# Feed-forward of a decoder step: the group of two, its PSUM readers and the places of its jobs

## The chip, the cores and the metric

The kernel runs on one core of one Trainium2 chip. The metric is the device time of one execution in microseconds (us), as the median over runs.

## What is computed

One step of a decoder of four layers over 544 columns (512 prompt tokens, 8 requests of 4 new tokens), in fp32. Each layer is a token mixer (convolution, latent attention, retention, convolution) and a gated feed-forward part, each behind an rmsnorm and with a residual add. The change touches the feed-forward part alone:

```python
def _swiglu(h, w1, w3, w2):
    return (jax.nn.silu(h @ w1) * (h @ w3)) @ w2
xp = xp + _swiglu(_rmsnorm(xp, norm_ffn[i]), ffn_w1[i], ffn_w3[i], ffn_w2[i])   # D_MODEL 1024, D_FF 2816
```

Here `w1` is the gate, `w3` the value and `w2` the down product.

## The kernel before, in words

`x` is held transposed in SBUF, 8 tiles of 128 rows by 544 columns. Every fp32 product is made of three matmuls of rounded halves: a weight tile is split by ACT into `wh` (a cast, L485) and by DVE into `wl` (a subtraction, L473), and the product is high by high, low by high and high by low.

The feed-forward part of a layer (`ffn`) is written as one list of **jobs**. A job is one product with all that belongs to it: a load, `sums` (DVE, sums of weight blocks, L580), `high` (the ACT cast of its weights), `low` (the DVE subtraction), `run` (the matmuls) and `after` (the instructions that read its PSUM result). `step(i)` emits job i: loads for job i+6, sums for i+3, its matmuls, then the cast for job i+2, the readers of job i-1, the low half for job i+2. A job with `soon` set has its own readers emitted at the end of its own step; one with `late` set has the readers of the job ahead of it emitted first. `in_order` keeps PE, DVE and ACT in exactly the order in which the jobs are emitted.

The 22 blocks of 128 hidden units are worked off as: four in the plain way (`plain`), their down product, a group of four (`quad`), then in the loop of `ffn` the four jobs of the down product of that group with the 14 jobs of a **group of two** between them, then two more groups of four with their down products. A `quad` group makes 7 products in place of 8 (Strassen's scheme, `four`), once for the gate and once for the value. In the order of the jobs these are products 1, 5, 6, 3, 7, 2, 4 of the scheme:

- The first three write PSUM and are copied to SBUF by ACT (L587: `u1`, `p5`, `u2`). The others go through `put`: for the gate an add on DVE (L638) and a Silu on ACT (L640), for the value an add and a multiplication on DVE (L650, L652), a cast `gh` on ACT (L653) and, one step later, `gl` on DVE.
- Product 6 adds onto the PSUM place of product 1, product 3 onto that of product 5, product 7 onto that of product 6. So each of them has to wait until the reader of the earlier one is done.
- In the group of two (`nt=1`) a job has 12 matmuls and its PSUM places are the two banks of one tile (`pair`): products 1, 6, 7, 4 in bank 0, products 5 and 3 in bank 1. In a group of four (`nt=2`) a job has 24 matmuls and the two places are two tiles. A job of the down product has 48 matmuls (24 ahead of each of its two adds into `x`, L299).

Below, the jobs of the group of two are called job 1 to job 14 (gate 1 to 7, value 8 to 14), the four down jobs between them D1 to D4, and the jobs of the next group of four, which follow, Q1, Q2, Q3, Q4. Before, the order is D1, jobs 1 to 4, D2, jobs 5 to 8, D3, jobs 9 to 11, D4, jobs 12 to 14, Q1. All four layers have this stretch once.

The functions that the diff touches:

Of the kernel before, what the change touches and what calls it, by code (L numbers as in the profile page):

```python
# [136 lines left out]
class Trunk:  # L137
# [306 lines left out]
    def ffn(self, l, last, order):  # L444
# [15 lines left out]
        with ExitStack() as es:  # L460
# [14 lines left out]
            class Job:  # L475

                load = sums = high = low = after = fill = staticmethod(lambda: None)
                late = soon = False

            def weights(job, src, nk, w):  # L480

                def high():
                    job.w = tuple(self.wsp.tile([P, 1024], FR, tag="ws", name="w" + n)[:, :nk * w]
                                  .rearrange("p (k c) -> p k c", k=nk) for n in "hl")
                    nc.scalar.copy(job.w[0], src())  # L485
                job.high, job.low = high, lambda: low(job.w[1], src(), job.w[0])
# [60 lines left out]
            def product(out, c, w, first):  # L547
                wh, wl = w
                bh, bl = blocks[c]
                for t in range(wh.shape[-1] // P):  # L550
                    m = slice(t * P, (t + 1) * P)
                    for i, (a, b) in enumerate(((wh, bh), (wh, bl), (wl, bh))):
                        for k in range(4):
                            nc.tensor.matmul(out[:, t, :HF], lhsT=a[:, k, m], rhs=b[:, k, :],  # L554
                                             start=(first and i == 0 and k == 0), stop=(i == 2 and k == 3),
                                             skip_group_check=True)

            def four(w, f, put, nt):

                a, ps, kept = {}, {}, {}  # L560
                v = lambda x: x[:, :, :HF]

                def load():
                    if nt == 1:
                        for i, n in enumerate(("1", "2")):
                            r = bp.tile([P, 1024], F, tag="A", name="raw", bufs=4).rearrange("p (k c) -> p k c", k=4)
                            nc.sync.dma_start(r, w[:, i * 4:(i + 1) * 4, f * P:f * P + 256])
                            a["1" + n], a["2" + n] = r[:, :, :P], r[:, :, P:]
                        return
                    r = self.rawp.tile([P, 2048], F, tag="raw", name="raw").rearrange("p (k c) -> p k c", k=4)  # L570
                    nc.sync.dma_start(r, w[:, 0:4, f * P:f * P + 512])
                    a["11"], a["21"] = r[:, :, :256], r[:, :, 256:]
                    for i, n in enumerate(("22", "12")):
                        a[n] = bp.tile([P, 1024], F, tag="A", name="raw", bufs=4).rearrange("p (k c) -> p k c", k=4)
                        nc.sync.dma_start(a[n], w[:, 4:8, f * P + 256 - 256 * i:f * P + 512 - 256 * i])

                def whole(out, op, x, y):
                    def sums():
                        a[out] = self.xsp.tile([P, 1024], F, tag="xs", name="S")[:, :nt * 512].rearrange("p (k c) -> p k c", k=4)
                        op(a[out], a[x], a[y])  # L580
                    return sums
                add, sub = nc.vector.tensor_add, nc.vector.tensor_sub

                def copy(name, p):
                    def after():
                        t = kept[name] = self.scr(name).rearrange("p (t n) -> p t n", t=2)[:, :nt]
                        nc.scalar.copy(t, v(ps[p]))  # L587
                    return after

                for c, n, sums, p, first, after in (  # L590
                        ("1", "11", None, "x2", True, copy("u1", "x2")),
                        ("5", "S1", whole("S1", add, "21", "22"), "x3", True, copy("p5", "x3")),
                        ("6", "S2", whole("S2", sub, "S1", "11"), "x2", False, copy("u2", "x2")),
                        ("3", "S4", whole("S4", sub, "12", "S2"), "x3", False, lambda: put("12", v(ps["x3"]), kept["u2"])),
                        ("7", "S3", whole("S3", sub, "11", "21"), "x2", False, lambda: put("22", v(ps["x2"]), kept["p5"])),
                        ("2", "12", None, "x1", True, lambda: put("11", v(ps["x1"]), kept["u1"])),
                        ("4", "22", None, "x2", False, lambda: put("21", v(ps["x2"]), None))):
                    job = Job()
                    if c == "1":
                        job.load = load  # L600
                    if sums:
                        job.sums = sums
                    weights(job, lambda n=n: a[n], 4, nt * P)

                    def run(job=job, c=c, p=p, first=first):
                        if first and nt == 1:
                            if p != "x3":
                                ps["pair"] = self.pair(p)
                            i = int(p == "x3")
                            ps[p] = ps["pair"][:, i:i + 1]  # L610
                        elif first:
                            ps[p] = (self.duo if p == "x2" else self.pair)(p)
                        product(ps[p], c, job.w, first)
                    job.run, job.after = run, after
                    yield job

            def quad(f, gs, nt=2):
# [24 lines left out]
                def value(which, ps, add):  # L642
# [12 lines left out]
                    if which == "21":  # L655
                        gs.extend((G[p][0][:, j, :], G[p][1][:, j, :]) for p in "12" for j in range(nt))
                yield from four(w1, f, gate, nt)
                yield from four(w3, f, value, nt)


# [52 lines left out]
            jobs, gs = [], []  # L713
# [5 lines left out]
            while f < FF // P:  # L719
                gs, ahead = ahead, []  # L720
                jobs.extend(quad(f, gs))
                f += 4
                if last and f == FF // P:
                    break
                back = list(down(f0, f - f0, gs))
                if f0 == 4:
                    two = list(quad(f, ahead, 1))
                    for i, n in enumerate((4, 4, 3, 3)):
                        jobs.append(back[i])
                        jobs.extend(two[:n])  # L730
                        del two[:n]
                    f0, f = f, f + 2
                else:
                    jobs.extend(back)
                    f0 = f
# [14 lines left out]
            def made(i, *what):  # L750
                for n in what:
                    if i < len(jobs) and (i, n) not in done:
                        done.add((i, n))
                        getattr(jobs[i], n)()

            def caught_up():
                todo, behind[:] = behind[:], []
                for x in todo:
                    x()

            def step(i):
                job = jobs[i]
                made(i + 6, "load")
                made(i + 3, "sums")
                if job.late:
                    jobs[i - 1].after()
                    caught_up()
                job.run()
                caught_up()
                made(i + 2, "high")  # L770
                if i and not job.late and not jobs[i - 1].soon:
                    jobs[i - 1].after()
                made(i + 2, "low")
                if job.soon:
                    job.after()
                job.fill()
            for i in range(6):
                made(i, "load")
            for i in range(3):
                made(i, "high", "low")  # L780
            step(0)
            with self.in_order(mybir.EngineType.PE, mybir.EngineType.DVE, mybir.EngineType.Activation):
                for i in range(1, len(jobs)):
                    step(i)
                if not jobs[-1].soon:
                    jobs[-1].after()
                caught_up()
# [1151 lines left out]
```

## Time and profile before

| | |
|---|---|
| median of 3 runs | 2788.76 us (2784.15 to 2789.15) |
| profiled execution | 2775.68 us, span of its instructions 2773.8 us |
| mean granted TensorE clock | 0.994 |
| PE busy | 2707.9 us, 98% of the span |
| DVE, ACT busy | 1942.5 us (70%), 1196.7 us (43%) |
| this stretch in the first layer | job 1 starts at 351.34 us, Q3 at 400.38 us |

PE is the engine of the matmuls, PEld its weight loads, DVE the vector engine, ACT the scalar engine. A row of a timeline has its start in the span, its duration, the engine, the line, the operation, what it writes and reads, and in brackets how long the engine was idle before it and what ended that. PE rows overlap, since matmuls are pipelined: from start to start is what one costs.

### The profile page before, as it was taken

The page shows a single profiled execution, that of the slowest core. Times are in us where ns is not written, and L with a number is a line of the kernel's source. Part 1 is how long each engine was busy: PE and PEld are TensorE (multiplying, and loading weights), DVE is VectorE, ACT ScalarE, POOL GpSimd, SP SyncE. Part 2 cuts the span into 40 slices and gives each one's busy share as a digit, 9 for nine tenths or more (in the row PEclk, how much of TensorE's full clock was granted, in tenths as well). Part 3 has the DMA queues.
Part 4 walks back from the last instruction along what each step waited for, and adds up shares of the span by engine and source line. Part 5 has one row for each costly group of instructions (what it writes and reads, how often), then busy time and mean ns, then how long its engine had stood idle before and what let it go on. Part 6 is the DMA issues. An engine that isn't in the chain of part 4 may idle for free.

```text
span 2773.8 us, 52206 instructions
## 1 busy us (share of the span) xinstructions
PE 2707.9 (98%) x22294; PEld 2544.2 (92%) x22294; DVE 1942.5 (70%) x2878; ACT 1196.7 (43%) x1793; POOL 138.1 (5%) x233
## 2 busy tenths in 40 slices
PE   8999999999899999999999999999999999999998
PEld 7989999997679999999888888899999998999998
DVE  6987765776665867677656565786767798776576
ACT  4155443444454344344534343534434425444345
POOL 1000000021430000000101000000000000000000
PEclk9999999999999999999999999999999999999999
DMA  5544223233333233322525343422331453422322
GB/s 161 184 136 138 92 88 96 91 91 116 87 114 107 77 92 100 99 69 87 194 94 178 109 163 122 142 94 92 96 103 63 128 192 128 143 84 88 98 82 86
DMA packets 222300, 312.47 MB, mean 113 GB/s; under 512 B 15295, under 2 KB 153868, under 8 KB 222038
## 3 DMA queue, kind: packets, MB, share of 16 engines
q1 hardware_dynamic: 209164, 266.84, 30.4%
q0 software_dynamic: 12608, 40.44, 4.2%
q8 instruction: 175, 2.87, 0.4%
q10 hardware_dynamic: 298, 1.88, 0.2%
q14 instruction: 55, 0.45, 0.1%
HBM read 278.78 MB, written 30.85 MB: 112 GB/s over the span
## 4 chain that ended last, share of the span: by engine, by line
PE 89%; DVE 6%; ACT 2%; DMA 1%; issue 1%; another core or an unknown queue 0%; ACTq 0%; DVEq 0%
PE x L554 26%; PE p L216 24%; PE pg L216 7%; PE pqk L216 3%; PE pa L216 3%; PE pwo L216 3%; PE po L216 2%; PE pw L216 2%; PE pd L216 2%; PE pv L1586 1%; PE pv L1587 1%; PE pv L1588 1%; PE ob L1821 1%; DVE cc L881 1%; DMA raw<-in_ffn_w 1%
## 5 line engine op out<-in xcount | busy, mean ns | idle before, releaser
L485 ACT CAST wh<-raw 128x1024 fp32r<-128x1024 f32 (+2 forms) x244 | 239.2, 980 | 365.8 <-PE p L216 200.5
L554 PE MATMUL x<-Bh,wh 128*128 128x272 f32 x2016 | 336.8, 289 | 11.0 <-ACT u L587 5.8
L554 PE MATMUL x<-Bh,wl 128*128 128x272 f32 x2016 | 334.6, 288 | 0.0
L554 PE MATMUL x<-Bl,wh 128*128 128x272 f32 x2016 | 334.5, 288 | 0.0
L473 DVE TENSOR_TENSOR wl<-raw,wh 128x1024 fp32r<-128x1024 f32 (+2 forms) x244 | 276.4, 1133 | 76.5 <-ACT wh L485 74.5
L196 ACT CAST wh<-raw 128x1024 fp32r<-128x1024 f32 (+2 forms) x170 | 160.6, 948 | 367.5 <-PE pg L216 77.8
L554 PEld LDWEIGHTS x<-Bh,wh 128*128 128x128 f32 x2016 | 283.9, 188 | 15.2 <-ACT u L587 7.6
L216 PE MATMUL p<-gl,wh 128*128 128x272 f32 x1344 | 296.0, 288 | 1.0 <-DVE gl L473 1.0
L216 PE MATMUL p<-gh,wh 128*128 128x272 f32 x1344 | 296.9, 289 | 0.0
L216 PE MATMUL p<-gh,wl 128*128 128x272 f32 x1344 | 296.2, 288 | 0.0
L554 PEld LDWEIGHTS x<-Bh,wl 128*128 128x128 f32 x2016 | 283.9, 188 | 0.0
L554 PEld LDWEIGHTS x<-Bl,wh 128*128 128x128 f32 x2016 | 283.9, 188 | 0.0
L485 ACT CAST wh<-S 128x1024 fp32r<-128x1024 f32 (+1 forms) x160 | 154.6, 966 | 268.1 <-PE p L216 139.2
L299 DVE TENSOR_TENSOR x<-p,x 128x544 f32<-128x544 f32 x152 | 109.9, 723 | 191.6 <-PE p L216 191.4
L197 DVE TENSOR_TENSOR wl<-raw,wh 128x1024 fp32r<-128x1024 f32 (+2 forms) x170 | 185.4, 1094 | 72.3 <-ACT wh L196 52.9
L473 DVE TENSOR_TENSOR wl<-S,wh 128x1024 fp32r<-128x1024 f32 (+1 forms) x160 | 178.1, 1115 | 71.2 <-ACT wh L485 71.2
L216 PEld LDWEIGHTS p<-gl,wh 128*128 128x128 f32 x1344 | 218.1, 188 | 1.9 <-DVE gl L473 1.9
L216 PEld LDWEIGHTS p<-gh,wh 128*128 128x128 f32 x1344 | 218.0, 188 | 1.2 <-ACT gh L518 0.9
L216 PEld LDWEIGHTS p<-gh,wl 128*128 128x128 f32 x1344 | 217.2, 189 | 0.0
L216 PE MATMUL pg<-xs,wh 128*128 128x272 f32 x1024 | 178.8, 292 | 5.1 <-ACT wh L196 5.1
L216 PE MATMUL p<-xs,wh 128*128 128x272 f32 x1024 | 172.6, 290 | 5.6 <-DVE t L295 5.6
L216 PEld LDWEIGHTS pg<-xs,wh 128*128 128x128 f32 x1024 | 147.7, 190 | 13.2 <-issue 7.3
(540 smaller groups left out, 5323.7 us busy)
## 6 DMA issues: line engine op xcount, KB each, us to landing
raw<-in_ffn_w SPq DMA_DIRECT2D x78, 1024.0 KB
raw<-in_ffn_w SPq DMA_DIRECT2D x88, 512.0 KB
raw<-in_conv_w_pw SPq DMA_DIRECT2D x28, 1024.0 KB
state<-in_state_ret SPq DMA_DIRECT2D x32, 512.0 KB
out_ret_state_sample<-state POOLq DMA_DIRECT2D x32, 512.0 KB
S<-ud SPq DMA_DIRECT2D x48, 280.0 KB
raw<-in_ffn_w SPq DMA_DIRECT2D x16, 768.0 KB
raw<-in_ret_w_v SPq DMA_DIRECT2D x8, 1024.0 KB
```

Source lines behind the costliest of these rows:

```text
L196: self.nc.scalar.copy(hv, raw)
L197: self.nc.vector.tensor_sub(lv, raw, hv.bitcast(F))
L216: nc.tensor.matmul(ps[:M, h, :HF], lhsT=w[:, k, :], rhs=x[:, h * HF:(h + 1) * HF], start=(j == 0 and i == 0), stop=(j == n - 1 and i == 2))
L299: self.nc.vector.tensor_add(x, ps[:, :, :HF], x)
L473: nc.vector.tensor_sub(out, a, flat(h))
L485: nc.scalar.copy(job.w[0], src())
L554: nc.tensor.matmul(out[:, t, :HF], lhsT=a[:, k, m], rhs=b[:, k, :], start=(first and i == 0 and k == 0), stop=(i == 2 and k == 3), skip_gr ...
L881: nc.vector.scalar_tensor_tensor(out=cc[m][:, a:z], in0=U[:, m, k + a:k + z], scalar=taps[:, m, k:k + 1], in1=cc[m][:, a:z], op0=ALU.mult, ...
L1586: nc.tensor.matmul(out, lhsT=ah, rhs=bh, start=start, stop=False)
L1587: nc.tensor.matmul(out, lhsT=ah, rhs=bl, start=False, stop=False)
L1588: nc.tensor.matmul(out, lhsT=al, rhs=bh, start=False, stop=stop)
L1821: nc.tensor.matmul(s["ob"][q * 32:(q + 1) * 32, :], lhsT=s["qm"][:, e, q * 2 + r, :], rhs=ts[q // 2][:, q % 2, :], start=(q > 0 and r == 0 ...
```

## The change

It does two things. Jobs of a group of two get a flag `short`, and where the job ahead is `short`, its readers are emitted ahead of the cast for job i+2 instead of behind it. And the 14 jobs stand 5, 4, 3, 2 behind D1, D2, D3, D4, where they stood 4, 4, 3, 3.

```diff
-                late = soon = False
+                late = soon = short = False
...
-                    job.run, job.after = run, after
+                    job.run, job.after, job.short = run, after, nt == 1
                     yield job
...
-                    for i, n in enumerate((4, 4, 3, 3)):
+                    for i, n in enumerate((5, 4, 3, 2)):
                         jobs.append(back[i])
                         jobs.extend(two[:n])
                         del two[:n]
...
                 job.run()
                 caught_up()
+                mine = not i or job.late or jobs[i - 1].soon
+
+                if not mine and jobs[i - 1].short:
+                    jobs[i - 1].after()
+                    mine = True
                 made(i + 2, "high")
-                if i and not job.late and not jobs[i - 1].soon:
+                if not mine:
                     jobs[i - 1].after()
                 made(i + 2, "low")
```

On **PE**, in the first layer, at the end of the first run of short jobs (`x2_4184` is the PSUM pair of the gate, `p2` the result of a down job; a row is a run of equal matmuls). Before, jobs 3 and 4 and the start of D2:

```order
L554 MATMUL x2_4184<-Bh_3473,wh_4197 128x272 x4
L554 MATMUL x2_4184<-Bl_3474,wh_4197 128x272 x4
L554 MATMUL x2_4184<-Bh_3473,wl_4198 128x272 x4
L554 MATMUL x2_4184<-Bh_3345,wh_4213 128x272 x4
L554 MATMUL x2_4184<-Bl_3346,wh_4213 128x272 x4
L554 MATMUL x2_4184<-Bh_3345,wl_4214 128x272 x4
L216 MATMUL p2_4263<-gh_4042,wh_4237 128x272 x2
L216 MATMUL p2_4263<-gl_4043,wh_4237 128x272 x2
L216 MATMUL p2_4263<-gh_4042,wl_4238 128x272 x2
```

With the change:

```order
L554 MATMUL x2_4184<-Bh_3473,wh_4197 128x272 x4
L554 MATMUL x2_4184<-Bl_3474,wh_4197 128x272 x4
L554 MATMUL x2_4184<-Bh_3473,wl_4198 128x272 x4
L554 MATMUL x2_4184<-Bh_3345,wh_4217 128x272 x4
L554 MATMUL x2_4184<-Bl_3346,wh_4217 128x272 x4
L554 MATMUL x2_4184<-Bh_3345,wl_4218 128x272 x4
L554 MATMUL x2_4184<-Bh_3406,wh_4239 128x272 x4
L554 MATMUL x2_4184<-Bl_3407,wh_4239 128x272 x4
L554 MATMUL x2_4184<-Bh_3406,wl_4240 128x272 x4
L216 MATMUL p2_4282<-gh_4042,wh_4257 128x272 x2
L216 MATMUL p2_4282<-gl_4043,wh_4257 128x272 x2
L216 MATMUL p2_4282<-gh_4042,wl_4258 128x272 x2
```

Job 5 (`Bh_3406`) has moved ahead of D2; in the same way job 9 has moved ahead of D3 and job 12 ahead of D4.

On **ACT**, at the seam between the group of two and the next group of four (`wh` of 128x1024 are the weights of Q1 to Q4, `gh` the reader of a job of the group of two, `u1_4713` the copy of Q1). Before:

```order
L485 CAST wh_4611<-raw_4473 128x1024
L653 CAST gh_4570<-hid_4316 128x272
L485 CAST wh_4634<-S_4596 128x1024
L653 CAST gh_4570<-hid_4316 128x272
L485 CAST wh_4670<-S_4619 128x1024
L653 CAST gh_4570<-hid_4316 128x272
L485 CAST wh_4710<-S_4642 128x1024
L587 COPY u1_4713<-x2_4644 128x544
```

With the change:

```order
L485 CAST wh_4616<-raw_4477 128x1024
L653 CAST gh_4529<-hid_4275 128x272
L485 CAST wh_4638<-S_4600 128x1024
L653 CAST gh_4529<-hid_4275 128x272
L485 CAST wh_4672<-S_4620 128x1024
L485 CAST wh_4710<-S_4642 128x1024
L587 COPY u1_4713<-x2_4644 128x544
```

The three `gh` of before are those of jobs 12, 13, 14; the two with the change are those of jobs 13 and 14. So the cast of Q2 stood behind the reader of job 12 and now stands behind that of job 13, and the cast of Q3 stood behind that of job 13 and now stands behind that of job 14.

On **DVE**, the same seam, with the change (`S` are sums of weights, `v` and `hid` the add and the multiplication of a job of the group of two):

```order
L473 TENSOR_TENSOR wl_4617<-raw_4477,wh_4616 128x1024
L580 TENSOR_TENSOR S_4620<-S_4600,raw_4477 128x1024
L650 TENSOR_TENSOR v_4634<-x1_4602,u1_4411 128x272
L652 TENSOR_TENSOR hid_4275<-v_4634,hid_4275 128x272
L473 TENSOR_TENSOR wl_4639<-S_4600,wh_4638 128x1024
L580 TENSOR_TENSOR S_4642<-raw_4481,S_4620 128x1024
L473 TENSOR_TENSOR gl_4530<-hid_4275,gh_4529 128x272
L652 TENSOR_TENSOR hid_4275<-x2_4379,hid_4275 128x272
L473 TENSOR_TENSOR wl_4673<-S_4620,wh_4672 128x1024
```

The kinds of rows and their order are here those of before (which has one `gl` more, that of job 12, ahead of `v`); `wl_4639`, the low half of Q2, stands right behind job 13's multiplication in both.

## Rows read from the trace of the kernel before

**Rows 1.** The page: the span and PE's busy time.
```profile
span 2773.8 us, 52206 instructions
...
PE 2707.9 (98%) x22294; PEld 2544.2 (92%) x22294; DVE 1942.5 (70%) x2878; ACT 1196.7 (43%) x1793; POOL 138.1 (5%) x233
```

**Rows 2.** What ended PE's idle time before L554, whole kernel: us, times.
```profile
  ACT u L587: 5.8, 8
  ACT p L587: 3.8, 8
  DVE v L650: 1.3, 4
```

**Rows 3.** Timeline of PE, first layer: jobs 1, 2, 3, D2, 5, 13, 14, Q1, Q2, Q3.
```profile
351.34 0.67 PE L554 MATMUL x<-Bh,wh 128*128 128x272 f32 x4
...
352.85 0.66 PE L554 MATMUL x<-Bh,wh 128*128 128x272 f32 x4
...
354.99 0.77 PE L554 MATMUL x<-Bh,wh 128*128 128x272 f32 x4 [0.47 <-ACT u L587]
...
358.83 0.41 PE L216 MATMUL p<-gh,wh 128*128 128x272 f32 x2
...
364.85 0.67 PE L554 MATMUL x<-Bh,wh 128*128 128x272 f32 x4
...
389.66 0.67 PE L554 MATMUL x<-Bh,wh 128*128 128x272 f32 x4
...
391.67 0.74 PE L554 MATMUL x<-Bh,wh 128*128 128x272 f32 x4 [0.34 <-DVE v L650]
...
393.24 0.66 PE L554 MATMUL x<-Bh,wh 128*128 128x272 f32 x4
...
396.24 0.66 PE L554 MATMUL x<-Bh,wh 128*128 128x272 f32 x4
...
400.38 0.77 PE L554 MATMUL x<-Bh,wh 128*128 128x272 f32 x4 [0.98 <-ACT u L587]
```

**Rows 4.** Timeline of ACT, first layer: copies of jobs 1 and 3, then the seam.
```profile
354.55 0.39 ACT L587 COPY u<-x 128x272 f32<-128x272 f32 x1 [0.95 <-PE x L554]
...
359.03 0.39 ACT L587 COPY u<-x 128x272 f32<-128x272 f32 x1 [1.34 <-PE x L554]
...
395.48 0.42 ACT L653 CAST gh<-hid 128x272 fp32r<-128x272 f32 x1 [2.07 <-DVE hid L652]
395.81 1.05 ACT L485 CAST wh<-S 128x1024 fp32r<-128x1024 f32 x1
...
399.73 0.60 ACT L587 COPY u<-x 128x544 f32<-128x544 f32 x1
```

**Rows 5.** Timeline of DVE, first layer, from D4's second add on.
```profile
388.36 0.72 DVE L299 TENSOR_TENSOR x<-p,x 128x544 f32<-128x544 f32 x1 [2.28 <-PE p L216]
389.00 0.43 DVE L473 TENSOR_TENSOR gl<-hid,gh 128x272 fp32r<-128x272 f32 x1
...
393.05 1.22 DVE L580 TENSOR_TENSOR S<-S,raw 128x1024 f32<-128x1024 f32 x1
394.18 0.44 DVE L473 TENSOR_TENSOR gl<-hid,gh 128x272 fp32r<-128x272 f32 x1
394.53 0.44 DVE L650 TENSOR_TENSOR v<-x,u 128x272 f32<-128x272 f32 x1
395.00 0.44 DVE L652 TENSOR_TENSOR hid<-v,hid 128x272 f32<-128x272 f32 x1
395.36 1.22 DVE L473 TENSOR_TENSOR wl<-S,wh 128x1024 fp32r<-128x1024 f32 x1
396.50 1.22 DVE L580 TENSOR_TENSOR S<-raw,S 128x1024 f32<-128x1024 f32 x1
```

**Rows 6.** Stretches in the last convolution layer: length, PE busy, granted clock, DMA.
```profile
2398.00:2402.00 4.00, 1.89 (x16) 1.00 0.01 4
2402.00:2408.00 6.00, 6.00 (x37) 0.72 0.01 3
```

## The prediction

> **What bounds the kernel now.** I read the page first. PE is busy for 98% of the span [rows 1], so nothing shortens this kernel but PE's idle time, and whatever adds to that adds to the time. The change leaves every matmul as it is. So I next asked what PE waits for ahead of the line that the group of two uses: 10.9 us in 20 waits over the four layers [rows 2], which is five waits a layer. In PE's timeline each layer has the same five at the same distances: ahead of jobs 3, 4, 11, 14 and ahead of Q3.
>
> What one costs is seen from start to start. A short job takes 1.50 (351.34 to 352.85), a down job 6.02 (358.83 to 364.85), Q1 takes 3.00 [rows 3]. Job 3 starts 2.14 behind job 2, so 0.64 is lost, and its own first matmuls run 0.10 longer than unhindered ones (0.77 for 0.66): 0.74 a wait, for each of jobs 3, 4 and 11. Job 14 starts 2.01 behind job 13, which is 0.50, and with the longer start (0.74) some 0.57. Q3 starts 4.14 behind Q2, which is 1.14 [rows 3]. Together 3.9 us a layer, 15.7 us in all. That is all there is to gain here.
>
> **What the waits wait for.** Job 3 adds onto the place that holds job 1's product, so it waits for job 1's copy. Job 1 ended at 352.85, but its copy starts only at 354.55 [rows 4], although ACT was idle for 0.95 ahead of it. What it waited for is the end of job 2 (352.85 + 1.50, and some 0.2 until the result is out). Job 2 writes the other bank of the same PSUM tile. The same holds for job 3's copy at 359.03, which comes 0.2 behind the end of job 4 at 358.83. So inside a run of short jobs a copy goes when the next job has ended, wherever on ACT it is issued. The Trainium skill ("PSUM — Partial Sum Buffer", PSUM bank collisions raise a hardware error) wants PSUM guarded by bank and quadrant, which would let job 1 be read while job 2 fills the other bank. The trace does not agree for this program: the copy at 354.55 was held back by the other bank. By the rule the four such waits below, 4 x 0.74, would fall out of the sum (rival 1); by the row they stay, and I take the row.
>
> **The change, part by part** (first layer, on the clock of the trace).
>
> *Jobs 1 to 5.* Jobs 3 and 4 wait as before. Job 5 adds onto the place of job 3. Before, D2 lay between, and the copy was long done; now job 5 follows job 4 at once and needs the copy that starts 0.2 behind job 4's end. That is a new wait of 0.74. The run ends at 351.34 + 5 x 1.50 + 3 x 0.74 = 361.06.
>
> *D2.* Its weights are cast behind that copy: at 359.03 + 0.33 (as the cast at 395.81 comes 0.33 behind the start of the short `gh` [rows 4]) for 1.05, until 360.41, then its low half on DVE for 1.22 [rows 5], until 361.65. D2 wants the low half four matmuls, 0.5, into itself, at 361.56. A tie, which I put at 0.1; it lies between 0 (the low half comes a little sooner) and 0.3.
>
> *Jobs 6 to 9, D3, jobs 10 to 12, D4.* Job 11 had its wait because job 9 and 10 stood side by side behind D3; now D3 stands between jobs 9 and 10, and the copy of job 9 is done under it: 0.74 gone. Job 12 follows job 11 at once, and waits for the copy of job 10: 0.74 new. D4's weights stand behind that copy, a tie again, 0.1. So 361.06 + 6.12 (D2) + 6.00 + 6.02 (D3) + 4.50 + 0.74 + 6.12 = 390.56 is the end of D4. Jobs 13 and 14 then take 3.00 without a wait, since the reader that job 14 needs, job 12's, is done under D4 (0.57 gone). Q1 starts at 393.56, 0.3 later than before [rows 3].
>
> *The seam.* Here the new place of the casts costs. DVE has a full queue from D4's second add on: before, it works without a gap from 388.36 (0.2 behind D4's end) to 396.50 and beyond [rows 5]. ACT's casts of Q2 and Q3 ran ahead of that queue; the cast of Q2 stood behind the reader of job 12. Now it stands behind the `gh` of job 13, and that waits for DVE's multiplication. DVE's row of work from start to start [rows 5]: the add 0.64, sums of weights 1.13, a low half of Q 1.14, `gl` 0.35, `v` 0.47. So the add at 390.76, the first sum 391.40, `gl` 392.53, the low half of Q1 392.88, the second sum 394.02, `v` 395.15, `hid` 395.62. `gh` starts 0.48 behind `hid`, the cast 0.33 behind `gh` [rows 4]: 396.43, and ends at 397.48. Q2 is due at 393.56 + 3.00 = 396.56 and starts 0.05 behind the cast, at 397.53: 0.97 lost, 0.10 for its start, and 0.1 as its low half (397.52 + 1.22 = 398.74) is due at 398.63. Q2 ends at 400.73.
>
> DVE has meanwhile stood still from 396.1 to 397.52, since the low half of Q2 is its next instruction. That idle second pushes on: the third sum 398.66, `gl` 399.79, `hid` of job 14 400.14, `gh` 400.62, the cast of Q3 400.95 to 402.0. Behind it in ACT's queue stands the cast of Q4, which was made possible by the third sum, for 1.0, and only then the copy of Q1, 0.60 long, on which Q3 waits: 403.6. Q3 started at 400.38 before [rows 3]. From there on the jobs are 3 us long, and ACT and DVE keep ahead as before.
>
> *What costs nothing.* The loads: SP's queue has the same transfers in the same order, and each is emitted six jobs ahead of its use; they shift with PE, and no wait of rows 2 is ended by one. ACT's other readers (the Silu of jobs 4 to 7) now stand ahead of casts that are due two jobs or a down job later. If that cover failed, a late cast would cost what Q2's does.
>
> **The sum.** A layer loses 4 x 0.74 + 2 x 0.1 + 1.17 (Q2) + 2.9 (Q3) = 7.2, where it lost 3.9. By the clock of the trace it is 403.6 against 400.38, **3.2 us a layer, 12.8 us in all**. The profiled execution took 2775.68 and would take 2788.5; it lies 13 us below the median of the runs, and I add the same to the median: **2801.6 us**, 0.46% slower. A change of 0.2% (5.6 us) is about what a measurement of this kernel can tell. Should the queue of DVE run 0.6 earlier than I have it, 2.6 a layer are left, 2799; with 0.3 at D2 and D4 and the seam 0.4 later, 4.2 a layer, 2805.5.
>
> **The rivals.**
>
> 1. *The readers run ahead (not slower).* If a copy that is issued ahead of the cast starts at the end of its own job, jobs 3, 4, 5 and 12 lose nothing. D4's end and DVE's queue behind it move up together, so the seam stays as it is: 7.2 - 2.96 against 3.9, 0.3 a layer, 2790. It decides whether the copies of jobs 1 to 3 start less than 0.3 behind the end of their own job. Against it speak both copies in rows 4. I give it 0.04. The skill's rule above speaks for it.
> 2. *The casts of Q2 and Q3 are in time (no change).* If DVE gets to job 13 a good second earlier, the seam is as before, and only new waits against old ones count: 2.96 + 0.2 + 1.14 against 3.9, 0.4 a layer, 2790.4. Against it: DVE has no gap there to be earlier in [rows 5]. 0.08. Rivals 1 and 2 together would make the kernel faster: 0.2 + 1.14 against 3.9, -2.6 a layer, 2778.5; 0.03.
> 3. *Only Q2 is late.* If DVE's idle second is made up before job 14, Q3 keeps its 1.14: 1.6 a layer, 2795. Against it: the low half of Q2 is queued ahead of all that Q3 needs. 0.12.
> 4. *The clock falls too.* In the last convolution layer PE was busy for 1.89 of 4 us, and over the next 6 us the granted clock was 0.72 [rows 6], a mix of 1.2 and 2.4 GHz which by 0.28 x 6 costs 1.7 us. At Q3's wait that would make it 4.9 a layer, 2808.4. Against it: PE works for most of the time from Q1 to Q3. 0.05. The Trainium skill ("TensorE: Matmul & The Clock Gate", Why this matters for your kernels) warns of idle gaps between bursts of matmuls, which speaks against the change; rows 6 agree that the clock can fall in this kernel.
> 5. *The change does nothing.* Excluded: the order on ACT and PE shows every step moved.
>
> **How the numbers follow.** My forecast has 0.68. Faster by over 0.2% are rivals 1 and 2 together, 0.03; within 0.2% is either of them alone, 0.12; slower are the forecast and rivals 3 and 4, 0.85. The range takes in rival 3, the bounds of the forecast and rival 4, and leaves out the rest, 0.15: 2791 to 2809. The forecast's own range is 2797 to 2806.
>
> **What would show it.** In the changed profile: copies of jobs 1, 2 and 3 start 0.2 behind the end of the next job; PE waits ahead of jobs 3, 4, 5, 12 by 0.47 each and no more ahead of 11 and 14; DVE has two idle times of about 1.4 ahead of the low halves of Q2 and Q3, ended by ACT's cast; PE waits about 1 us for the cast ahead of Q2 and 2.5 to 3 us for the copy `u` ahead of Q3. It is wrong if copies start at the end of their own jobs, or if PE's idle time ahead of Q2 is nil.

## The result, and the profile after

The change makes the kernel slower: 2801.26 us (median of 5 runs, 2798.55 to 2803.53) against 2786.86 (5 runs, 2784.15 to 2789.15), a ratio of 1.0052 with a 95% interval of 1.0037 to 1.0066. That is 14.5 us by the ratio; 12.8 were forecast.

The page of the changed kernel, the span and the busy times, answers to [rows 1]:

```profile
span 2799.5 us, 52222 instructions
...
PE 2720.8 (97%) x22294; PEld 2552.8 (91%) x22294; DVE 1942.8 (69%) x2878; ACT 1194.9 (43%) x1793; POOL 137.7 (5%) x233
```

DVE and ACT do the same work in a longer span; their cost has not moved, only their order. PE's busy time has grown by 12.9 us over the same 22294 matmuls: in part these are matmuls at a lower clock, which are busy for longer (last section). What ended PE's idle time ahead of L554 (us, times), against [rows 2]:

```profile
  ACT u L587: 15.4, 16
  ACT wh L485: 3.4, 4
  ACT p L587: 1.9, 4
```

20 waits have become 24. `p` has halved (job 11's wait is gone), `v` has gone (job 14's), a wait for a cast is new, and `u` has grown from 5.8 to 15.4. PE's timeline in the first layer shows the new ones at the seam: job 1 for its start, then jobs 13 and 14, Q1, Q2 with its first thirds, Q3 and Q4.

```profile
354.76 0.67 PE L554 MATMUL x<-Bh,wh 128*128 128x272 f32 x4
...
394.24 0.67 PE L554 MATMUL x<-Bh,wh 128*128 128x272 f32 x4
...
395.75 0.67 PE L554 MATMUL x<-Bh,wh 128*128 128x272 f32 x4
...
397.25 0.66 PE L554 MATMUL x<-Bh,wh 128*128 128x272 f32 x4
...
401.26 0.77 PE L554 MATMUL x<-Bh,wh 128*128 128x272 f32 x4 [0.85 <-ACT wh L485]
401.87 0.66 PE L554 MATMUL x<-Bl,wh 128*128 128x272 f32 x4
402.52 0.77 PE L554 MATMUL x<-Bh,wl 128*128 128x272 f32 x4
...
407.21 1.05 PE L554 MATMUL x<-Bh,wh 128*128 128x272 f32 x4 [2.42 <-ACT u L587]
...
411.85 0.66 PE L554 MATMUL x<-Bh,wh 128*128 128x272 f32 x4
```

Jobs 13 and 14 run without a wait. Q1 starts at 397.25, so Q2 is due at 400.25; it waits for its cast until 401.26 and once more, 0.15, for its low half (402.52), with a second slow start. Q3 is due at 404.64 and starts at 407.21. From here on the **stretch** is the time from job 1's start to Q3's start. It is 52.45 with the change (354.76 to 407.21); before it was 49.04 [rows 3]. All four layers have the same waits of 0.47 (jobs 3, 4, 5, 12), 0.85 and 2.42, so the stretch costs 3.4 us a layer, 13.6 in all.

ACT at the seam, against [rows 4]:

```profile
399.84 0.42 ACT L653 CAST gh<-hid 128x272 fp32r<-128x272 f32 x1 [4.55 <-DVE hid L652]
400.17 1.04 ACT L485 CAST wh<-S 128x1024 fp32r<-128x1024 f32 x1
404.34 0.42 ACT L653 CAST gh<-hid 128x272 fp32r<-128x272 f32 x1 [3.13 <-DVE hid L652]
404.66 1.99 ACT L485 CAST wh<-S 128x1024 fp32r<-128x1024 f32 x2
406.56 0.60 ACT L587 COPY u<-x 128x544 f32<-128x544 f32 x1
```

ACT sits idle for 4.55 and 3.13 us with a cast behind the reader that could have run in that time (where the places alone are changed, below, it does). DVE, against [rows 5]:

```profile
399.37 0.44 DVE L652 TENSOR_TENSOR hid<-v,hid 128x272 f32<-128x272 f32 x1
401.24 1.23 DVE L473 TENSOR_TENSOR wl<-S,wh 128x1024 fp32r<-128x1024 f32 x1 [1.43 <-ACT wh L485]
402.38 1.22 DVE L580 TENSOR_TENSOR S<-raw,S 128x1024 f32<-128x1024 f32 x1
403.52 0.44 DVE L473 TENSOR_TENSOR gl<-hid,gh 128x272 fp32r<-128x272 f32 x1
403.87 0.43 DVE L652 TENSOR_TENSOR hid<-x,hid 128x272 f32<-128x272 f32 x1
405.74 1.22 DVE L473 TENSOR_TENSOR wl<-S,wh 128x1024 fp32r<-128x1024 f32 x1 [1.43 <-ACT wh L485]
```

Before, the low half of Q2 started 0.36 behind job 13's `hid`, without a gap [rows 5]. Now DVE finishes `hid`, ACT makes `gh` and the cast, and only then DVE goes on: two gaps of 1.43 in the engine that is the bound at the seam.

The two profiled executions are 25.6 us apart (2775.68 and 2801.26), more than the medians. 13.6 of it is the stretch and 4.4 the clock at Q3 (last section). The rest lies outside the code that the change moves: 3.4 ahead of job 1 in the first layer (351.34 against 354.76) and 4.0 between the end of Q4 in the first layer and job 1 in the second (609.1 against 613.1). In the profiled execution of the places alone (2790.93, below) these two took 356.0 and 618.3, so they differ by some us from one profiled execution to the next although the code there is the same. The profiled execution of before is 11 us below the median of its runs, the changed one is at its median.

### The profile page after: what moved, and what is told of

Read it like the earlier page. It is cut to its first block, busy times and chain, and to the rows that moved or that the text cites. A ratio compares the mean times of both kernels' runs of the same rounds, so it can differ in the third digit from the quotient of the medians.

```text
span 2799.5 us, 52222 instructions
## 1 busy us (share of the span) xinstructions
PE 2720.8 (97%) x22294; PEld 2552.8 (91%) x22294; DVE 1942.8 (69%) x2878; ACT 1194.9 (43%) x1793; POOL 137.7 (5%) x233
## 4 chain that ended last, share of the span: by engine, by line
PE 83%; DVE 4%; ACT 2%; DMA 1%; issue 1%; another core or an unknown queue 0%; SPq 0%; ACTq 0%
PE x L554 26%; PE p L216 23%; PE pg L216 5%; PE pqk L216 3%; PE pwo L216 3%; PE po L216 2%; PE pa L216 2%; PE pd L216 1%; PE pv L1591 1%; PE pv L1592 1%; PE pv L1593 1%; PE ob L1826 1%; PE pw L216 1%; DMA raw<-in_ffn_w 1%; PE up L1830 1%
## 5 line engine op out<-in xcount | busy, mean ns | idle before, releaser
L554 PE MATMUL x<-Bh,wh 128*128 128x272 f32 x2016 | 339.0, 290 | 20.7 <-ACT u L587 15.4
L554 PE MATMUL x<-Bh,wl 128*128 128x272 f32 x2016 | 336.3, 289 | 0.0
L554 PE MATMUL x<-Bl,wh 128*128 128x272 f32 x2016 | 336.1, 289 | 0.0
L554 PEld LDWEIGHTS x<-Bh,wh 128*128 128x128 f32 x2016 | 285.3, 189 | 25.9 <-ACT u L587 18.9
L554 PEld LDWEIGHTS x<-Bh,wl 128*128 128x128 f32 x2016 | 284.9, 189 | 0.9 <-DVE wl L473 0.9
L554 PEld LDWEIGHTS x<-Bl,wh 128*128 128x128 f32 x2016 | 285.5, 189 | 0.0
```

## The experiments

The theory is that the seam carries the cost: readers ahead of casts make the casts of Q2 and Q3 wait for DVE. Its main rival is that the places 5, 4, 3, 2 carry it. The first four kernels ran together (the kernel before took 2786.59 beside them), the second four together at another time and on another chip (2756.55 beside them). The two differ by 1%, so each ratio is to the kernel before as it ran in the same group, and only ratios are compared.

### The places alone

```diff
-                    for i, n in enumerate((4, 4, 3, 3)):
+                    for i, n in enumerate((5, 4, 3, 2)):
```

> The jobs stand 5, 4, 3, 2, the readers stay behind the casts. Measured as the stretch from the start of job 1 to the start of Q3 in each layer: 49.04 us before, 52.44 with the whole change. Theory (the readers ahead of the casts cost at the seam, the places cost nearly nothing): PE waits ahead of jobs 3, 4, 5, 12 by 0.47 each, none ahead of Q2, and ahead of Q3 about 1.4, since D4's adds lie one job closer to Q1: stretch 49.6, time 2 to 3 us above before. Rival (the places cost it: only two short jobs are left as cover between D4 and Q1): Q2 waits for its cast, stretch 51.5 or more, time 10 us or more above before.

Measured: 2787.05 us, ratio 1.0001 (0.9992 to 1.0010): no change. PE's idle time ahead of L554, whole kernel:

```profile
  ACT u L587: 10.8, 16
  ACT p L587: 1.9, 4
```

No wait for `wh` ahead of Q2. The waits are those expected (jobs 3, 4, 5, 12 at 0.47, Q3 at 1.27), and the stretch is 49.50. DVE at the seam works through, with Q2's low half right behind `hid`:

```profile
400.16 0.44 DVE L652 TENSOR_TENSOR hid<-v,hid 128x272 f32<-128x272 f32 x1
400.52 1.22 DVE L473 TENSOR_TENSOR wl<-S,wh 128x1024 fp32r<-128x1024 f32 x1
```

ACT casts the weights of Q2 as soon as their sum is there, over 3 us ahead of the reader of job 13:

```profile
397.26 1.06 ACT L485 CAST wh<-S 128x1024 fp32r<-128x1024 f32 x1 [1.12 <-DVE S L580]
400.64 0.42 ACT L653 CAST gh<-hid 128x272 fp32r<-128x272 f32 x1 [2.32 <-DVE hid L652]
```

So the places by themselves are not the cause. They trade job 11's and job 14's waits for those of jobs 5 and 12, and a Q3 that waits 0.29 longer.

### The readers alone

```diff
-                    for i, n in enumerate((5, 4, 3, 2)):
+                    for i, n in enumerate((4, 4, 3, 3)):
```

(against the changed kernel)

> The readers of a short job go ahead of the next cast, the jobs stand 4, 4, 3, 3 as before. Theory (the casts of Q1, Q2, Q3 wait behind the readers of jobs 12, 13, 14, and DVE stands still for each): three idle times of about 1.4 us on DVE ended by a cast, Q2 about 2 us late, Q3 more: stretch 53, 4 us above before's 49.04, time 16 us above before, and 4 more where the clock falls at Q3. Rival (the places cost it): stretch below 50, time at most 4 us above before.

Measured: 2810.88 us, ratio 1.0090 (1.0076 to 1.0104), about 25 us slower: worse than the whole change. DVE at the seam:

```profile
396.71 1.22 DVE L473 TENSOR_TENSOR wl<-raw,wh 128x1024 fp32r<-128x1024 f32 x1 [1.44 <-ACT wh L485]
...
401.68 1.23 DVE L473 TENSOR_TENSOR wl<-S,wh 128x1024 fp32r<-128x1024 f32 x1 [1.43 <-ACT wh L485]
...
406.18 1.23 DVE L473 TENSOR_TENSOR wl<-S,wh 128x1024 fp32r<-128x1024 f32 x1 [1.43 <-ACT wh L485]
```

Three short jobs behind D4 make three such gaps, one for each of Q1, Q2, Q3, where two short jobs make two. The stretch is 54.55, 5.5 a layer against 4 expected. Q2 is 1.97 late (401.70 for 396.73 + 3.00), as expected. Not expected was what is lost ahead of Q1: from job 1 to Q1 it is 43.63 for 41.90 before, a wait ahead of job 8 (0.28 idle, for the add of job 6 on DVE) and one inside D3 (0.33, for its low half) among it. The clock fell at Q3 in three of the four layers here too (Q3 took 4.59, 4.63, 3.12 and 4.63 from its start to Q4's). So the new places soften what the readers cost. The two halves of the change do not add up; they interact at the seam.

### The whole change with the seam spared

```diff
-                if not mine and jobs[i - 1].short:
+                if not mine and jobs[i - 1].short and (jobs[i + 2].short or jobs[i + 2].soon):
```

> The whole change, but the readers of a short job go ahead of the next cast only where that cast is for a short job or a down job; ahead of the casts of Q2 and Q3 the order of before is kept. Theory (the seam carries the cost): no DVE idle time of 1.4 us at the seam, Q2 in time, Q3 1 to 1.5 us late: stretch 49.8, time 3 us above before, and no fall of the clock at Q3. Rival (readers ahead of casts cost inside the runs of short jobs as well): stretch above 51.

Measured: 2788.38 us, ratio 1.0007 (0.9998 to 1.0016), stretch 49.98. PE's idle time ahead of L554, and DVE at the seam:

```profile
  ACT u L587: 11.0, 16
  ACT p L587: 1.9, 4
```

```profile
398.16 0.44 DVE L652 TENSOR_TENSOR hid<-v,hid 128x272 f32<-128x272 f32 x1
398.52 1.22 DVE L473 TENSOR_TENSOR wl<-S,wh 128x1024 fp32r<-128x1024 f32 x1
```

The gaps on DVE at the seam, the wait ahead of Q2 and the fall of the clock at Q3 are gone; Q3 waits 1.33. With these places the reader order inside the runs of short jobs gains nothing and costs little: with the places alone at 49.50, 0.48 a layer is left for it, of which 0.42 are the waits of D2 and D4 for their low halves (from job 1 to Q1 it is 42.07 with the places alone and 42.49 with the change). So most of the change's cost sits in the casts of Q2 and Q3: putting those back in their old order takes the stretch from 52.45 to 49.98.

### A tile of its own for products 5 and 3

```diff
-                            if p != "x3":
+                            if p != "x1":
                                 ps["pair"] = self.pair(p)
-                            i = int(p == "x3")
+                            i = int(p == "x1")
```

(against the kernel before; `x1` is the place of product 2, which before is the first bank of a second tile)

> The kernel before, but products 5 and 3 of a group of two (x3) get a PSUM tile of their own, which they share with product 2 (x1) where products 1, 6, 7, 4 (x2) shared it with them: the same amount of PSUM. Theory (a copy waits for the next job because that job writes the same tile): copies of jobs 1 to 3 start 0.2 us behind their own job or right behind the cast ahead of them, the waits ahead of jobs 3, 4 and 11 are gone, those ahead of job 14 and Q3 stay: stretch 46.8, time 9 us below before. Rival (the copy waits for something else, such as the order of PE's signals): stretch 49.0, no change. Rival (ACT and DVE are the bound there): the waits shrink but move behind casts, stretch 48, 4 us below before.

Measured: 2777.78 us, ratio 0.9963 (0.9949 to 0.9976), about 10 us faster, and the stretch is 46.82, where 46.8 was expected. The whole kernel's PE idle time ahead of L554:

```profile
  ACT u L587: 3.9, 4
  DVE v L650: 1.3, 4
```

And ACT in the first layer, where job 1 runs from 353.19 to 354.70, with the copies of jobs 1, 2 and 3:

```profile
355.35 0.38 ACT L587 COPY u<-x 128x272 f32<-128x272 f32 x1
...
356.91 0.37 ACT L587 COPY p<-x 128x272 f32<-128x272 f32 x1
...
357.97 0.38 ACT L587 COPY u<-x 128x272 f32<-128x272 f32 x1
```

The copy of job 1 starts while job 2 still runs (until 356.20), right behind the cast ahead of it, and job 3 waits for nothing. So in this program the wait goes by the PSUM tile: what held a copy back was the next job's matmuls into the other bank of the same tile. Neither the cast in front of the copy nor the order of PE's signals was the cause, so issuing the copy ahead of the cast could not take these waits away.

### The copy of Q1 ahead of the cast of Q4

```diff
-                    job.run, job.after, job.short = run, after, nt == 1
+                    job.run, job.after, job.short = run, after, nt == 1 or c == "1"
```

(against the changed kernel)

> The whole change, and the copy of product 1 of a group of four (Q1 at the seam) goes ahead of the next cast as well. Theory (Q3 waits for the copy of Q1, which stands on ACT behind the casts of Q3 and Q4): the cast of Q4 no longer counts, so Q3's wait is about 1.0 us shorter, Q2's stays: stretch 51.5 for 52.44, time 4 us below the changed kernel, and up to 4 more if the shorter wait keeps the clock up at Q3. Rival (Q3 is late by DVE's sums and not by ACT's order): stretch 52.4, no difference from the changed kernel.

The edit holds for product 1 of every group of four, not at the seam alone. Measured: ratio 1.0039 (1.0025 to 1.0053), about 11 us slower than the kernel before. Q3's wait is 1.47 idle for 2.42, the stretch 51.51, both as expected. But Q4 now waits too:

```profile
  ACT u L587: 11.6, 16
  ACT wh L485: 3.4, 4
  ACT p L587: 3.0, 8
```

`p` has 4 waits more, 0.28 each ahead of Q4. So a part of the wait is handed on. At Q3 the clock stayed at its upper level in all four layers (granted 1.00). From job 1 to the end of Q4, the four layers together took 232.6 us in this profiled execution and 238.6 in that of the change. But the step of the whole kernel from 1.0052 to 1.0039 is within the intervals: that the whole kernel gains is not shown. It is shown that about 1 us of Q3's wait was the cast of Q4 in front of the copy.

### The whole change with tiles of their own

The edit is that of the tiles, made in the changed kernel.

> The whole change with x3 in a PSUM tile of its own, shared with x1 instead of x2. Theory (the two costs are apart: the tile's guard inside the runs of short jobs, DVE's standing still at the seam): the waits ahead of jobs 3, 4, 5, 12 are gone, those ahead of Q2 (0.85 idle) and Q3 (2.42 idle) stay as they were: stretch 49.4, time about 2 us above the kernel before, 5 with the clock's fall at Q3. Rival (with copies on time, DVE and ACT are ahead at the seam too): stretch 47, 8 us below the kernel before.

Measured: ratio 1.0019 (1.0010 to 1.0028), about 5 us slower; stretch 49.02. PE's idle time ahead of L554:

```profile
  ACT u L587: 9.7, 4
  ACT wh L485: 3.2, 4
```

All waits of the short jobs are gone, those of D2 and D4 for their low halves too (which takes the stretch below the 49.4 expected), and those of Q2 and Q3 stay nearly as they were (0.79 and 2.41). The stretch is that of before; the clock fell at Q3 in two of the four layers (4.63 and 4.46 from Q3's start to Q4's for 3.11), which is 2.9 us in this profiled execution. This is rival 1 made true, and it ends where rival 1 said, near the kernel before: the seam is a cost by itself.

### Tiles of their own, and only Q1's copy ahead

```diff
-                    job.run, job.after, job.short = run, after, nt == 1
+                    job.run, job.after, job.short = run, after, nt == 2 and c == "1"
```

(with the tiles' edit and the places 4, 4, 3, 3)

> The kernel before with x3 in a tile of its own, and only the copy of product 1 of a group of four goes ahead of the next cast. Theory: Q3's wait of 0.98 idle shrinks to about 0.1, the rest is as with tiles of their own alone: stretch 45.9 for 46.8, time 12 to 13 us below the kernel before. Rival (Q3 is late by DVE): stretch 46.8, 9 us below.

Measured: ratio 0.9954 (0.9941 to 0.9968), about 13 us faster; stretch 45.88. Only job 14's wait is left:

```profile
  DVE v L650: 1.3, 4
```

The stretch is 0.94 shorter than with the tiles alone, as expected; the intervals of the two ratios overlap.

### The same with the places 5, 4, 3, 2

> As the last one, but the jobs stand 5, 4, 3, 2 (readers of short jobs behind the casts). Theory (the places free job 14, and with tiles of their own cost nothing ahead of jobs 5 and 12): only a wait of 0.3 to 0.5 ahead of Q3 is left: stretch 45.5, time 13 to 15 us below the kernel before. Rival (five short jobs side by side are more than ACT and DVE can feed): waits for casts ahead of jobs 4 and 5, stretch 46.5 or more, 10 us below the kernel before at most.

Measured: ratio 0.9948 (0.9934 to 0.9961), about 14 us faster than the kernel before; stretch 45.61. PE's idle time ahead of L554 is down from 10.9 us to

```profile
  ACT u L587: 1.3, 4
```

This has the lowest ratio of all that ran, and beats both kernels. Five short jobs side by side are fed in time. That the places add to the version ahead of it is not shown, since the two intervals overlap.

## Why the prediction was right, point by point

- **The copies.** They start when the next job has ended, as said, and the tile experiment shows why. The waits ahead of jobs 3, 4, 5, 12 are there at 0.47 idle each, those ahead of 11 and 14 are gone.
- **D2 and D4.** Put at 0.1 each, they measured 0.21 (D2 took 6.23, from 364.49 to 370.72, for 6.02). The cast and the low half came when reckoned (the low half was done 0.55 behind D2's start, and due at 0.50), but PE lost more than the 0.05 it was late. The bound of 0.3 held it.
- **Q2.** 1.17 forecast, 1.39 measured: 1.01 to its start, and 3.38 in place of 3.00 from its start to its end, for two slow starts and the wait for its low half.
- **DVE's two gaps.** 1.4 each forecast, 1.43 measured.
- **Q3.** 2.9 forecast, 2.57 measured. This term was over-sized: I gave the casts of Q3 and Q4 2.05 us together, and they took 1.90 until the copy started (404.66 to 406.56); and Q2 itself ended later than I had it, which takes from the wait behind it. From Q2's start to job 14's `hid` on DVE it was 2.61 forecast and 2.61 measured (401.26 to 403.87).
- **The sum.** 3.2 us a layer forecast, 3.4 measured in the stretch; 12.8 us in all forecast, 14.5 measured (10.3 to 18.4 by the interval of the ratio). That the median of 2801.26 lies so close to the 2801.6 forecast is luck: the kernel before came out 1.9 below the median that I added to, and the two medians lie 14.4 apart where 12.8 was forecast. In the profiled execution the stretch (13.6) and the clock (4.4) make 18.0, which the interval still holds; how often the clock fell in the other runs is not on record.
- **Rival 4** I gave 0.05, and it came in three of four layers. The step that failed there is "PE works for most of the time from Q1 to Q3" as an argument that the clock would stay. Its price (1.7) was near what it cost where it fell (1.3 to 1.5), and the forecast left this term out.
- **Rivals 1 to 3** did not occur. Rival 1's condition was met only with the tile changed, rival 2's only with the seam spared and with the places alone. Rival 3's, a late Q2 and a Q3 that loses no more than before, was met with none of them.

## What to carry to other kernels

Ask what an instruction really waits for before issuing it earlier: here the copies waited for a neighbour's matmuls in the same PSUM tile, and another tile gave 10 us, where neither the order of the readers nor the places had taken these waits away. Where the order on an engine is fixed, as here, an instruction that waits for a busy engine must not stand ahead of one that feeds that same engine: ACT's cast behind DVE's `hid` stopped DVE itself, 1.43 us each time. The two halves of a change should be tried apart: here one was neutral, and the other was worse than both together.

## What the runs showed of the hardware that was not expected

The clock fell at Q3's wait, in three layers of four. Each row is a part of the changed kernel's span, with its length, PE's busy time, granted clock, DMA share and GB/s. The first row is the time from Q1 up to Q3 in the first layer; the others are the time around Q3 in the first, second, third and fourth layer.

```profile
398.00:407.00 9.00, 5.95 (x44) 1.00 0.01 2
407.00:410.50 3.50, 3.29 (x15) 0.57 0.32 93
...
1080.00:1084.00 4.00, 3.66 (x18) 0.58 0.40 118
...
1987.00:1991.00 4.00, 3.71 (x18) 0.61 0.38 116
...
2575.00:2579.00 4.00, 3.21 (x25) 1.00 0.25 69
```

After 9 us with PE busy for 5.95 the granted clock fell: 0.57 over 3.5 us is a mix of the two levels, 2.4 and 1.2 GHz, most of it the lower one. In the fourth layer it stayed at the upper level, although the waits there are the same to 0.01 us. Where it fell, Q3 took 4.64 from its start to Q4's (407.21 to 411.85) instead of the 3.13 that it took before. Over the four layers this makes 4.4 us. So a wait of 2.42 us cost up to 1.5 us more behind it, and whether it does is not settled by the waits alone.

The other runs bear this out. PE waited 2.41 to 2.43 us ahead of Q3 in twelve places: four with the change, four with the readers alone, four with the change and tiles of their own. The clock fell behind eight of them (three, three and two). In the other seven kernels, the one before among them, the same wait was 0.03 to 1.48 us, and the clock fell behind none of these 28: Q3's first 3.1 us have a granted clock of 1.00 in each. What sets the eight apart from the four is not shown.
